# A softmax attention kernel: two and four of sixteen exponential blocks on VectorE in turn, one transposition step a unit, and a wait of GpSimd's product for VectorE's add

## The chip, the cores and the metric

The kernel runs on one core of a Trainium2 chip. The metric is the device time of one execution in microseconds (us), the median over several runs. A core has TensorE (PE in the profile; PEld is its loading of weights), VectorE (DVE), ScalarE (ACT), GpSimd (POOL) and SyncE (SP), each with a queue of its own that it works off in order. SBUF is the on-chip memory of all of them, PSUM the memory that TensorE writes its products to.

## The reference

Grouped-query attention: 32 query heads of 64 dimensions, 8 key and value heads, so four query heads share one of them. For each of 8 batches and 512 positions:

```python
batch, seq, n_heads, n_kv_heads, dim = 8, 512, 32, 8, 64
...
scores = np.einsum('bhqd,bhkd->bhqk', Q, K_expanded) * scale
weights = np.exp(scores - np.max(scores, axis=-1, keepdims=True))
weights = weights / (np.sum(weights, axis=-1, keepdims=True) + 1e-10)

output = np.einsum('bhqk,bhkd->bhqd', weights, V_expanded)
```

Inputs and output are float32.

## The kernel before

The kernel leaves the maximum out (exp without it gives the same quotient while nothing overflows) and checks on the way that the sums and V stay in bounds; if they do not, a slow general path recomputes everything. Here only the fast path runs.

**Units and jobs.** A unit is one batch and two of its key heads, with the eight query heads that use them: 32 units, four a batch. A unit is two jobs (64 in all, numbered j): job j has one key head and its four query heads as two pairs i = 0 and 1. The scores of a job are 16 blocks of 128 keys by 512 queries, and each block is to be exponentiated. Two blocks (m = 0, 1) share a PSUM tile of 128 × 1024.

**Two ways to the exponential.** ScalarE does most blocks: `act_tile(j, n)` has TensorE write scores to one of two PSUM tiles `s_ps`, and ScalarE writes exp of them to the SBUF tile `pt` (one ACTIVATE of 1024, or of 512 where a tile has a single block left). VectorE and GpSimd do the first blocks of pair 1, with integer arithmetic on the bits of a 16-bit float:

- `exp_d`: TensorE writes scores into `d_ps`, VectorE scales them to an integer `u`;
- `exp_d2`: VectorE masks the low ten bits, `f = u & 1023`, and, from job 3 to 62, GpSimd at once computes `g` (an add and a multiply of f) and the product `w = g * f` (`exp_d3`, `correction`);
- `exp_d4`: VectorE adds, `pt = u + w`, one job later.

`taken(j)` says how many blocks go this way: two, or three in even jobs from job 10 on (`WIDE`). With three, the third block has a scores matmul and a u of its own, issued at the end of the job before, and ScalarE's tile beside it has one block of 512 elements.

**The rest of a job.** While the scores of job j are made, TensorE multiplies the weights of job j−1 with V: `pv(last, 0, ...)` and `pv(last, 1, ...)`, each 32 matmuls into the one PSUM tile `pv`; a column of ones in V gives the sums. `norm(last, i)` then runs on VectorE: a reciprocal of the sums (L336) and a multiplication into `osb` (L340); SyncE stores a unit when its last norm is issued. `trans_q` transposes a job's queries on TensorE into `d_ps` (eight transposes) and VectorE copies them to `qt` (L167), for job j + 2. `check_v` (L173) reduces a chunk of V to its maximum, `check_sums` (L304) tests the collected reciprocals every eighth job.

**Order.** The order on each engine is the order in which the program is written (`tc.manual_schedule()`); semaphores follow from the tiles. In the main loop a job runs, on VectorE: u; norm of the last job's pair 0; the copy of queries; the add of the last job; f of this job; norm of pair 1. So f, and GpSimd's g and w behind it, follow the add, which has waited for the last job's w:

```python
        if late and by_pool(last):
            exp_d4(last)
        check_sums()
        exp_d2(j)
```

GpSimd also issues the loads of Q, K and V, ahead of its g and w in a job. SyncE transposes K by DMA at the start of a batch's third unit, and stores. PSUM: two tiles `s_ps`, one `d_ps` (for the scores of VectorE's blocks and for transposes by turns), one `pv`, two banks each.

Of the kernel before, what the change touches and what calls it, by code (L numbers as in the profile page):

```python
# [12 lines left out]
BF16 = mybir.dt.bfloat16  # L13
FP16 = mybir.dt.float16
# [3 lines left out]
ALU = mybir.AluOpType  # L18
# [15 lines left out]
V_HI = 1.0e15  # L34


WIDE = lambda j: j >= 10 and j % 2 == 0


@with_exitstack  # L40
# [18 lines left out]
def fast_path(ctx, tc, Q, K, V, out, flag):  # L59
    nc = tc.nc  # L60
    B, S, H, D = Q.shape
# [3 lines left out]
    GP = KV // 2  # L65
# [65 lines left out]
    def d_tile():  # L131
        return d_pool.tile([128, 2, S], FP32, name="d_ps")
# [3 lines left out]
    def first_k(gp, swap, bank):  # L136
# [8 lines left out]
                nc.tensor.transpose(ps[:, sc, :], kn[0][:, sc, h:h + 2, :], ident)  # L145
        return lambda: nc.vector.tensor_copy(out=kt_first[:, gp, swap, :], in_=half_bank)  # L146

    def dma_k(b):
        kt[b] = kt_pool.tile([128, 2, GP, S], BF16, name="kt")
        for sc in range(SC):  # L150
            nc.sync.dma_start_transpose(
                out=kt[b][:, 0, :, sc * 128:(sc + 1) * 128],
                in_=kn[b][:, sc, :, :].rearrange("p g d -> p (g d)"),
            )
        for to, of in ((0, 64), (64, 0)):
            nc.sync.dma_start(out=kt[b][to:to + 64, 1, :, :], in_=kt[b][of:of + 64, 0, :, :])

    def trans_q(j, bank, lo=0, hi=NPAIR):
        u, g = divmod(j, 2)
        ps = bank.bitcast(BF16).rearrange("p (i sc c) -> p i sc c", i=NPAIR, sc=SC)  # L160
        for i in range(lo, hi):
            for sc in range(SC):
                h = g * HPG + 2 * i
                nc.tensor.transpose(ps[:, i, sc, :], qn[u][:, sc, h:h + 2, :], ident)  # L164
        if u not in qt:
            qt[u] = qt_pool.tile([128, 2, NPAIR, S], BF16, name="qt")
        return lambda: nc.vector.tensor_copy(  # L167
            out=qt[u][:, g, lo:hi, :], in_=ps[:, lo:hi, :, :].rearrange("p i sc c -> p i (sc c)")
        )

    def check_v(b, sc):
        n = b * SC + sc
        nc.vector.tensor_reduce(  # L173
            out=okv[:, n:n + 1], in_=vt[b % 2][:, sc, :, 0:D], op=ALU.max, axis=AX.XY,
            apply_absolute_value=True,
        )
# [4 lines left out]
    DPAIR = NPAIR - 1  # L181

    def taken(j):
        return 3 if WIDE(j) else 2

    def act_tiles(j):
        every = [(i, kc, m) for i in range(NPAIR) for kc in range(SC) for m in range(2)]
# [19 lines left out]
    def open_job(j):  # L207
        pt = pt_pool.tile([128, NPAIR, SC, 2, S], FP16, name="pt")
        jobs.setdefault(j, {}).update(pt=pt, pv={})

    def act_tile(j, n):
        group = act_tiles(j)[n]
        i, kc, lo = group[0]
        ps = s_pool.tile([128, 2, S], FP32, name="s_ps")
        for _, _, m in group:
            scores(j, ps[:, m, :], i, kc, m)
        nc.scalar.activation(  # L217
            out=jobs[j]["pt"][:, i, kc, lo:, :], in_=ps[:, lo:, :], func=EXP, scale=scale
        )

    def exp_d(j, lo, hi, ps):
        st = jobs.setdefault(j, {})
        if "u" not in st:
            for name, dtype in (("u", I16), ("f", I16), ("g", BF16), ("w", BF16)):
                st[name] = dve_pool.tile([128, 3, S], dtype, name=name + "16")[:, 0:taken(j), :]
        for n in range(lo, hi):
            scores(j, ps[:, n - lo, :], DPAIR, n // 2, n % 2)
        return lambda: nc.vector.tensor_scalar(  # L228
            out=st["u"][:, lo:hi, :], in0=ps[:, 0:hi - lo, :], scalar1=A_U, scalar2=B_U,
            op0=ALU.mult, op1=ALU.add,  # L230
        )
# [7 lines left out]
    def correction(engine, f, g, w):  # L239
        as_bits = engine is nc.gpsimd  # L240
        engine.tensor_scalar(  # L241
            out=g, in0=f, scalar1=-EXP_F1, scalar2=EXP_K * 2.0 ** (24 * as_bits),
            op0=ALU.add, op1=ALU.mult,
        )
        engine.tensor_tensor(out=w, in0=g, in1=f.bitcast(FP16) if as_bits else f, op=ALU.mult)  # L245

    def exp_d2(j):
        st = jobs[j]
        nc.vector.tensor_single_scalar(  # L249
            out=st["f"], in_=st["u"], scalar=1023, op=ALU.bitwise_and  # L250
        )
        if by_pool(j):
            exp_d3(j, nc.gpsimd)

    def exp_d3(j, engine):
        st = jobs[j]
        correction(engine, st["f"], st["g"], st["w"])

    def exp_d4(j):
        st = jobs[j]  # L260
        n = taken(j)
        nc.vector.tensor_tensor(  # L262
            out=st["pt"][:, DPAIR, :, :, :].rearrange("p kc m q -> p (kc m) q")[:, 0:n, :].bitcast(
                U16
            ),
            in0=st["u"],
            in1=st["w"],
            op=ALU.add,
        )
# [8 lines left out]
    def pv(j, i, lo, hi):  # L278
        st = jobs[j]
        u, g = divmod(j, 2)  # L280
        b, gp = divmod(u, GP)
        if lo == 0:

            if j < NJOB - 1:
                t = pv_pool.tile([128, 2, S], FP32, name="pv")
            else:
                t = d_tile() if i == 0 else s_pool.tile([128, 2, S], FP32, name="s_ps")
            t = t.rearrange("p m (qc c) -> p m qc c", qc=SC)
            st["pv"][i] = t[:, :, :, 0:D + 1]
        order = blocks(j, i)  # L290
        for n in range(lo, hi):
            kc, m, qc = order[n]
            nc.tensor.matmul(  # L293
                st["pv"][i][:, m, qc, :],
                st["pt"][:, i, kc, m, qc * 128:(qc + 1) * 128],
                vt[b % 2][:, kc, 2 * gp + g, :],
                start=(n < 2 * SC and qc == 0),
                stop=(n >= len(order) - 2 * SC and qc == SC - 1),
            )
# [108 lines left out]
    trans_q(0, bank[:, 0, :], 0, 1)()  # L408


    for j in range(NJOB):
        end = j == NJOB - 1
        last = j - 1
        late = last >= 0
        u, g = divmod(j, 2)
        b, gp = divmod(u, GP)
        open_job(j)
        if j == 1:

            nc.gpsimd.tensor_copy(out=gate, in_=jobs[0]["pt"][0:1, 0, SC - 1, 0, 0:1])  # L420
            load_q(2)
            load_q(3)
        if g == 0 and u >= 1 and u + 3 < NU:
            load_q(u + 3)
        if (gp, g) == (1, 0) and b + 1 < B:
            load_k(b + 1)
        if 3 <= 2 * gp + g < 3 + SC and b + 1 < B:
            load_v(b + 1, chunks=(2 * gp + g - 3,))
        if gp == 2 and g == 0 and b + 1 < B:
            dma_k(b + 1)  # L430

        cut = (4, 18) if taken(j) > 2 else (11, 19)
        act_tile(j, 0)
        if j == 0:
            trans_q(0, bank[:, 1, :], 1, NPAIR)()
            act_tile(j, 1)
            exp_d(j, 0, 2, d_tile())()
        else:
            exp_d(j, 0, 2, d_tile())()
            act_tile(j, 1)  # L440

        if j == 8:
            check_v(0, 0)
        if g == (b < B - 1) and j > 1:
            check_v(b, gp)
        if late:
            pv(last, 0, 0, 16)
        act_tile(j, 2)
        if late:
            pv(last, 0, 16, 32)  # L450
            norm(last, 0)
        act_tile(j, 3)

        reads = []
        if not end:
            bank = d_tile()

            ahead = (j + 1,) if j < 7 else (8, 9) if j == 7 else (j + 2,)
            for n, to in enumerate(ahead):
                if to < NJOB:  # L460
                    reads.append(trans_q(to, bank[:, n, :]))
            if j == 1:
                for swap in range(2):
                    reads.append(first_k(1, swap, bank[:, 1, swap * S // 2:]))
            elif j > 1 and b == 0 and gp + 1 < GP:
                reads.append(first_k(gp + 1, g, bank[:, 1, :]))
        else:
            pv(j, 0, 0, 16)
        for read in reads:
            read()  # L470
# [5 lines that stand above are left out]
        if not by_pool(j):  # L476
            exp_d3(j, nc.vector)
            exp_d4(j)
        act_tile(j, 4)
        if late:  # L480
            pv(last, 1, 0, cut[0])
        act_tile(j, 5)
        if not end and taken(j + 1) > 2:
            exp_d(j + 1, 2, taken(j + 1), bank[:, 1:2, :])()
        if late:
            pv(last, 1, *cut)
        act_tile(j, 6)
        if late:
            pv(last, 1, cut[1], 32)
            norm(last, 1)  # L490
            del jobs[last]
        if end:
            pv(j, 0, 16, 32)
            norm(j, 0)
            pv(j, 1, 0, 32)
            norm(j, 1)
# [118 lines left out]
```

## Time and profile before

| | |
|---|---|
| median of three runs | 423.73 us (423.22 to 424.65) |
| span of the profiled execution | 422.0 us |
| ScalarE busy | 404.2 us, 96% |
| TensorE matmul busy | 385.7 us, 91% (ends modelled) |
| VectorE busy | 344.9 us, 82% |
| GpSimd busy | 291.8 us, 69% |
| mean granted TensorE clock | 0.984 |

The profiled execution's own time is its span of 422.0 us from the first to the last instruction; what lies around it is the difference to the runs' times, 1.7 us to their median. Busy shares are means over the whole span. In the steady part an even and an odd job together take 12.50 us: on GpSimd's timeline, g of three blocks starts at 206.21, and g of two blocks at 199.99 and again at 212.48.

### The profile page before, as it was taken

Reading aid. Unit: us, or ns where it says so; the run is one execution under the profiler, and the core shown is the slowest. Engines: PE = TensorE matmul, PEld = TensorE weight load, DVE = VectorE, ACT = ScalarE, POOL = GpSimd, SP = SyncE. Lnnn points to the kernel's source line nnn. Section 1 sums busy time; section 2 is a strip of 40 time slices with the busy share of each in tenths; the row PEclk is TensorE's granted clock in tenths of the full one; section 3 lists DMA queues with packets and bytes.
Section 4 is the critical chain, followed back from the end, with each engine's and each line's share of the span. In section 5 each row is a group of like instructions: output and inputs, shape, how many; then the busy total and the mean of one; then the engine's idle time right before and its main releaser. Section 6 shows DMA issues by size and latency. Waiting matters only on the chain.

```text
span 422.0 us, 13063 instructions
## 1 busy us (share of the span) xinstructions
PE 385.7 (91%) x5689; PEld 233.6 (55%) x5689; DVE 344.9 (82%) x611; ACT 404.2 (96%) x449; POOL 291.8 (69%) x209
## 2 busy tenths in 40 slices
PE   6889999999999999999999999999999999999983
PEld 2446565555555555555555555555555555555552
DVE  2697788889888888888888888888989888898875
ACT  3899999999999999999999999999999999999992
POOL 8504656778758876787866887677885887666560
PEclk9599999999999999999999999999999999999998
DMA  9996986599967998499964999649996799642223
GB/s 97 177 139 159 217 165 151 70 207 187 191 151 99 216 198 160 133 198 133 229 150 116 206 163 255 157 69 200 157 225 155 122 206 207 148 123 101 102 91 115
DMA packets 91438, 66.95 MB, mean 159 GB/s; under 512 B 52080, under 2 KB 74608, under 8 KB 91376
## 3 DMA queue, kind: packets, MB, share of 16 engines
q0 software_dynamic: 56544, 25.17, 51.1%
q1 hardware_dynamic: 34832, 40.90, 34.5%
q8 instruction: 45, 0.74, 0.7%
q14 instruction: 17, 0.14, 0.1%
HBM read 50.33 MB, written 33.55 MB: 199 GB/s over the span
## 4 chain that ended last, share of the span: by engine, by line
ACT 54%; PE 36%; DVE 6%; issue 1%; POOL 1%; ACTq 0%; DVEq 0%; POOLq 0%
ACT pt L217 54%; PE s_ps L199 17%; PE pv L293 16%; PE d_ps L199 1%; DVE o_sb L340 1%; PE d_ps L164 1%; DVE pt L262 1%; DVE u L228 1%; DVE qt L167 1%; DVE w L245 0%; POOL q_nat L126 0%; DVE kt_first L146 0%; ACTq L217 0%; PE d_ps L143 0%; DVE f L249 0%
## 5 line engine op out<-in xcount | busy, mean ns | idle before, releaser
L217 ACT ACTIVATE pt<-s_ps 128x1024 f16<-128x1024 f32 (+1 forms) x448 | 402.9, 1066 | 9.1 <-PE s_ps L199 9.0
L293 PEld LDWEIGHTS <-pt 128*128 128x128 f16 x4096 | 144.2, 98 | 86.8 <-issue 50.4
L293 PE MATMUL pv<-v,pt 128*128 128x65 bf16 x4032 | 183.2, 195 | 2.6 <-DVE o_sb L340 1.6
L199 PE MATMUL s_ps<-qt,kt 64*128 64x512 bf16 x757 | 152.7, 384 | 19.9 <-ACT pt L217 15.4
L245 POOL TENSOR_TENSOR w<-g,f 128x1024 bf16<-128x1024 bf16 (+1 forms) x60 | 153.7, 2562 | 5.0
L241 POOL TENSOR_SCALAR g<-f 128x1024 bf16<-128x1024 int16 (+1 forms) x60 | 73.9, 1231 | 110.1 <-DVE f L249 110.1
L228 DVE TENSOR_SCALAR u<-d_ps 128x1024 int16<-128x1024 f32 (+1 forms) x91 | 96.2, 1058 | 1.1 <-PE d_ps L199 1.1
L340 DVE TENSOR_TENSOR o_sb<-pv,inv 128x512 f32<-128x512 f32 x125 | 86.5, 692 | 4.5 <-DVE inv L336 0.2
L199 PEld LDWEIGHTS <-kt 64*128 64x128 bf16 x896 | 49.0, 93 | 62.6 <-issue 35.0
L336 DVE RECIPROCAL inv<-pv 128x8 f32<-128x8 f32 x125 | 25.9, 207 | 55.8 <-PE pv L293 55.4
L262 DVE TENSOR_TENSOR pt<-u,w 128x1536 uint16<-128x1536 int16 (+1 forms) x64 | 50.9, 795 | 0.2
L167 DVE COPY qt<-d_ps 128x1024 bf16<-128x1024 bf16 (+1 forms) x65 | 44.3, 683 | 4.5 <-PE d_ps L164 2.9
L164 PE MATMUL d_ps<-ident,q_nat 128*128 128x128 bf16 x512 | 40.1, 222 | 1.1 <-DVE kt_first L146 0.9
L164 PEld LDWEIGHTS <-q_nat 128*128 128x128 bf16 x512 | 29.2, 98 | 15.8 <-issue 15.7
L199 PE MATMUL d_ps<-qt,kt 64*128 64x512 bf16 x139 | 31.4, 376 | 0.3
L249 DVE TENSOR_SCALAR f<-u 128x1536 int16<-128x1536 int16 (+1 forms) x64 | 30.8, 481 | 0.0
L111 POOL DMA_DIRECT2D v<-in_V_dram x32 | 29.0, 910 | 0.4 <-issue 0.4
L126 POOL DMA_DIRECT2D q_nat<-in_Q_dram x34 | 27.4, 806 | 1.5 <-DMA q_nat<-in_Q_dram 1.3
L199 PE MATMUL s_ps<-qt,kt_first 64*128 64x512 bf16 x112 | 23.7, 419 | 4.1 <-ACT pt L217 3.0
L173 DVE TENSOR_REDUCE okv<-v 128x1 f32<-128x512 bf16 x32 | 21.6, 675 | 0.0
L199 PEld LDWEIGHTS <-kt_first 64*128 64x128 bf16 x128 | 8.0, 95 | 12.2 <-issue 8.4
L103 POOL DMA_DIRECT2D k_nat<-in_K_dram x10 | 7.7, 770 | 1.0 <-POOLq L599 0.8
(40 smaller groups left out, 37.6 us busy)
## 6 DMA issues: line engine op xcount, KB each, us to landing
out_dram<-o_sb SPq DMA_DIRECT2D x31, 1024.0 KB, 6.9
q_nat<-in_Q_dram POOLq DMA_DIRECT2D x31, 512.0 KB, 6.3
k_nat<-in_K_dram POOLq DMA_DIRECT2D x7, 512.0 KB, 8.6
v<-in_V_dram POOLq DMA_DIRECT2D x28, 128.0 KB, 7.6
kt<-kt SPq DMA_DIRECT2D x14, 256.0 KB, 4.6
out_dram<-o_sb SPq DMA_DIRECT2D x4, 256.0 KB, 2.4
kt<-k_nat SPq DMA_TRANSPOSE x28, 5.6
v<-in_V_dram POOLq DMA_DIRECT2D x4, 96.0 KB, 7.8
```

Source lines behind the costliest of these rows:

```text
L111: nc.gpsimd.dma_start(out=vt[b % 2][:, sc, lo:hi, 0:D], in_=V[b, sc * 128:(sc + 1) * 128, lo:hi, :],)
L164: nc.tensor.transpose(ps[:, i, sc, :], qn[u][:, sc, h:h + 2, :], ident)
L167: return lambda: nc.vector.tensor_copy(out=qt[u][:, g, lo:hi, :], in_=ps[:, lo:hi, :, :].rearrange("p i sc c -> p i (sc c)"))
L199: nc.tensor.matmul(ps, keys[64 * m:64 * m + 64, g ^ m, kc * 128:(kc + 1) * 128], qt[u][64 * m:64 * m + 64, g, i, :], start=True, stop=True,)
L217: nc.scalar.activation(out=jobs[j]["pt"][:, i, kc, lo:, :], in_=ps[:, lo:, :], func=EXP, scale=scale)
L228: return lambda: nc.vector.tensor_scalar(out=st["u"][:, lo:hi, :], in0=ps[:, 0:hi - lo, :], scalar1=A_U, scalar2=B_U, op0=ALU.mult, op1=AL ...
L241: engine.tensor_scalar(out=g, in0=f, scalar1=-EXP_F1, scalar2=EXP_K * 2.0 ** (24 * as_bits), op0=ALU.add, op1=ALU.mult,)
L245: engine.tensor_tensor(out=w, in0=g, in1=f.bitcast(FP16) if as_bits else f, op=ALU.mult)
L249: nc.vector.tensor_single_scalar(out=st["f"], in_=st["u"], scalar=1023, op=ALU.bitwise_and)
L262: nc.vector.tensor_tensor(out=st["pt"][:, DPAIR, :, :, :].rearrange("p kc m q -> p (kc m) q")[:, 0:n, :].bitcast(U16), in0=st["u"], in1=st ...
L293: nc.tensor.matmul(st["pv"][i][:, m, qc, :], st["pt"][:, i, kc, m, qc * 128:(qc + 1) * 128], vt[b % 2][:, kc, 2 * gp + g, :], start=(n < 2 ...
L340: nc.vector.tensor_tensor(out=osb[u][:, :, h:h + 2, :].rearrange("p qc m d -> p m qc d"), in0=sums[:, :, :, 0:D], in1=inv[:, :, :, None].t ...
```

## The change

From job 8 to job 62 two new functions take the place of the loop's body, `two_job` for even and `four_job` for odd jobs; the jobs before and the last one run as they did, with `WIDE` gone (two blocks each).

- VectorE and GpSimd take two blocks in an even job and four in an odd one (9 to 61), so ScalarE has seven whole tiles and six. In a four_job the blocks go in two halves of two: each has its own scores, u, f, g and w; one add of four blocks follows in the next job.
- f is issued ahead of the add of the last job, not behind it. GpSimd's w waits for that add by an extra dependency (`behind`): in a four_job the first half's w for the add of two blocks, in a two_job w for the add of four.
- The queries of both jobs of the next unit are transposed in the even job, into both banks of `d_ps`, with one copy of 2048 elements (`copy_unit`) in place of two of 1024.
- The loads of Q and K are issued at the end of the even job, and one chunk of V at the end of each odd one. `check_v` runs in the even job. `check_sums` stands behind the second f of an odd job.

```diff
-WIDE = lambda j: j >= 10 and j % 2 == 0
+FOUR = lambda j: 9 <= j < 63 and j % 2 == 1
...
+    def copy_unit(u, both):
+        nc.vector.tensor_copy(
+            out=qt[u].rearrange("p g i s -> p (g i s)"),
+            in_=both.bitcast(BF16).rearrange("p n s -> p (n s)"),
+        )
...
     def taken(j):
-        return 3 if WIDE(j) else 2
+        return 4 if FOUR(j) else 2
...
+    def behind(this, other):
+        if this is not None and other is not None:
+            tc.add_manual_dep(
+                this.ins,
+                other.ins.name,
+                mybir.DependencyInfo(mybir.DependencyClass.Sync, mybir.DependencyReason.DATA),
...
+            )
+
+    def two_job(j):
+        u, last = j // 2, j - 1
+        b, gp = divmod(u, GP)
+        act_tile(j, 0)
+        exp_d(j, 0, 2, d_tile())()
+        act_tile(j, 1)
+        check_v(b, gp)
+        pv(last, 0, 0, 16)
+        act_tile(j, 2)
+        pv(last, 0, 16, 32)
+        norm(last, 0)
+        act_tile(j, 3)
+        both = d_tile()
+        if u + 1 < NU:
+            trans_q(j + 2, both[:, 0, :])
+        act_tile(j, 4)
+        if u + 1 < NU:
+            trans_q(j + 3, both[:, 1, :])
+        w = exp_d2(j)
+        behind(w, exp_d4(last))
+        if u + 1 < NU:
+            copy_unit(u + 1, both)
+        act_tile(j, 5)
+        pv(last, 1, 0, 16)
+        act_tile(j, 6)
+        pv(last, 1, 16, 32)
+        norm(last, 1)
+        del jobs[last]
+        if u + 3 < NU:
+            load_q(u + 3)
+        if gp == 1 and b + 1 < B:
+            load_k(b + 1)
+
+    def four_job(j):
+        last = j - 1
+        b, gp = divmod(j // 2, GP)
+        act_tile(j, 0)
+        exp_d(j, 0, 2, d_tile())()
+        w = exp_d2(j, 0, 2)
+        act_tile(j, 1)
+        pv(last, 0, 0, 16)
+        act_tile(j, 2)
+        pv(last, 0, 16, 32)
+        norm(last, 0)
+        behind(w, exp_d4(last))
+        act_tile(j, 3)
+        exp_d(j, 2, 4, d_tile())()
+        exp_d2(j, 2, 4)
+        check_sums()
+        act_tile(j, 4)
+        pv(last, 1, 0, 16)
+        act_tile(j, 5)
+        pv(last, 1, 16, 32)
+        norm(last, 1)
+        del jobs[last]
+        if b + 1 < B:
+            load_v(b + 1, chunks=(gp,))
...
+        if 8 <= j < NJOB - 1:
+            if gp == 2 and g == 0 and b + 1 < B:
+                dma_k(b + 1)
+            (four_job if FOUR(j) else two_job)(j)
+            continue
```

More of the change, by code (lines that the diff above doesn't have):

```diff
@@ L159, in trans_q @@
         u, g = divmod(j, 2)
+        if j >= NJOB:
+            return lambda: None
         ps = bank.bitcast(BF16).rearrange("p (i sc c) -> p i sc c", i=NPAIR, sc=SC)
@@ L224, in exp_d @@
             for name, dtype in (("u", I16), ("f", I16), ("g", BF16), ("w", BF16)):
-                st[name] = dve_pool.tile([128, 3, S], dtype, name=name + "16")[:, 0:taken(j), :]
+                st[name] = dve_pool.tile([128, 4, S], dtype, name=name + "16")[:, 0:taken(j), :]
         for n in range(lo, hi):
@@ L244, in correction, with exp_d2, exp_d3 @@
         )
-        engine.tensor_tensor(out=w, in0=g, in1=f.bitcast(FP16) if as_bits else f, op=ALU.mult)
-    def exp_d2(j):
+        return engine.tensor_tensor(
+            out=w, in0=g, in1=f.bitcast(FP16) if as_bits else f, op=ALU.mult
+        )
+    def exp_d2(j, lo=0, hi=None, behind=None):
         st = jobs[j]
+        hi = taken(j) if hi is None else hi
         nc.vector.tensor_single_scalar(
-            out=st["f"], in_=st["u"], scalar=1023, op=ALU.bitwise_and
+            out=st["f"][:, lo:hi, :], in_=st["u"][:, lo:hi, :], scalar=1023, op=ALU.bitwise_and
         )
         if by_pool(j):
-            exp_d3(j, nc.gpsimd)
-    def exp_d3(j, engine):
+            return exp_d3(j, nc.gpsimd, lo, hi)
+    def exp_d3(j, engine, lo=0, hi=None):
         st = jobs[j]
-        correction(engine, st["f"], st["g"], st["w"])
+        hi = taken(j) if hi is None else hi
+        return correction(engine, *(st[n][:, lo:hi, :] for n in ("f", "g", "w")))
     def exp_d4(j):
@@ L261, in exp_d4 @@
         n = taken(j)
-        nc.vector.tensor_tensor(
+        return nc.vector.tensor_tensor(
             out=st["pt"][:, DPAIR, :, :, :].rearrange("p kc m q -> p (kc m) q")[:, 0:n, :].bitcast(
@@ L408, in fast_path @@
     trans_q(0, bank[:, 0, :], 0, 1)()
+    def behind(this, other):
[4 more added lines that the diff above has]
+                mybir.DependencyInfo(mybir.DependencyClass.Sync, mybir.DependencyReason.DATA),
+                reason="these two hold up each other when they meet",
+            )
+    def two_job(j):
[54 more added lines that the diff above has]
+            load_v(b + 1, chunks=(gp,))
     for j in range(NJOB):
@@ L430, in fast_path @@
             dma_k(b + 1)
-        cut = (4, 18) if taken(j) > 2 else (11, 19)
+        cut = (11, 19)
         act_tile(j, 0)
@@ L440, in fast_path @@
             act_tile(j, 1)
-        if j == 8:
+        if j == 6:
             check_v(0, 0)
-        if g == (b < B - 1) and j > 1:
+        if g == 1 and 1 < j < 8:
             check_v(b, gp)
@@ L456, in fast_path @@
             bank = d_tile()
-            ahead = (j + 1,) if j < 7 else (8, 9) if j == 7 else (j + 2,)
+            ahead = (j + 1,) if j < 7 else (8, 9)
             for n, to in enumerate(ahead):
@@ L482, in fast_path @@
         act_tile(j, 5)
-        if not end and taken(j + 1) > 2:
-            exp_d(j + 1, 2, taken(j + 1), bank[:, 1:2, :])()
         if late:
```

## The prediction

> **What bounds the kernel now.** I read the page's busy line first, then the groups by form, then ScalarE's timeline, then one pair of jobs (an even and an odd one) on VectorE and GpSimd, last the list of waits.
>
> ```profile
> PE 385.7 (91%) x5689; PEld 233.6 (55%) x5689; DVE 344.9 (82%) x611; ACT 404.2 (96%) x449; POOL 291.8 (69%) x209
> ```
>
> ScalarE is the candidate. Its timeline, cut to two windows (start, length, count):
>
> ```profile
> 200.37 5.27 ACT L217 ACTIVATE pt<-s_ps 128x1024 f16<-128x1024 f32 x6
> 204.88 6.35 ACT L217 ACTIVATE pt<-s_ps 128x512 f16<-128x512 f32 x7
> ```
>
> Five whole tiles lie between 200.37 and 204.88: 0.90 us from start to start. The second row starts with a half tile and ends at 211.23; its last tile is 1.09 long, so six steps take 5.26, five of them whole (4.51): a half tile takes 0.75. A pair of jobs has 13 whole tiles and a half: 12.5 us. A window of one pair (212.48 to 224.98) has ScalarE busy for 12.50 of 12.50 us, VectorE for 10.49: ScalarE sets the pace.
>
> Prices, from the groups by form (busy us, mean ns | idle before):
>
> ```profile
> L245 POOL TENSOR_TENSOR w<-g,f 128x1024 bf16<-128x1024 bf16 x33 | 70.1, 2125 | 2.8
> L167 DVE COPY qt<-d_ps 128x1024 bf16<-128x1024 bf16 x63 | 43.5, 692 | 3.1 <-PE d_ps L164 1.5 <-PE d_ps L143 1.3 <-PE d_ps L145 0.3
> L241 POOL TENSOR_SCALAR g<-f 128x1024 bf16<-128x1024 int16 x33 | 34.3, 1039 | 66.7 <-DVE f L249 66.7
> L167 DVE COPY qt<-d_ps 128x512 bf16<-128x512 bf16 x2 | 0.8, 424 | 1.4 <-PE d_ps L164 1.4
> ```
>
> VectorE over the pair, in order of time:
>
> ```profile
> 201.58 1.21 DVE L228 TENSOR_SCALAR u<-d_ps 128x1024 int16<-128x1024 f32 x1
> 203.48 0.21 DVE L336 RECIPROCAL inv<-pv 128x8 f32<-128x8 f32 x1 [0.69 <-PE pv L293]
> 203.72 0.69 DVE L340 TENSOR_TENSOR o_sb<-pv,inv 128x512 f32<-128x512 f32 x1
> ...
> 204.96 0.68 DVE L262 TENSOR_TENSOR pt<-u,w 128x1024 uint16<-128x1024 int16 x1
> 205.56 0.55 DVE L249 TENSOR_SCALAR f<-u 128x1536 int16<-128x1536 int16 x1
> ...
> 207.87 1.22 DVE L228 TENSOR_SCALAR u<-d_ps 128x1024 int16<-128x1024 f32 x1
> 209.00 0.68 DVE L173 TENSOR_REDUCE okv<-v 128x1 f32<-128x512 bf16 x1
> 209.62 0.21 DVE L336 RECIPROCAL inv<-pv 128x8 f32<-128x8 f32 x1
> 209.86 0.69 DVE L340 TENSOR_TENSOR o_sb<-pv,inv 128x512 f32<-128x512 f32 x1
> 210.49 0.69 DVE L167 COPY qt<-d_ps 128x1024 bf16<-128x1024 bf16 x1
> 211.10 0.95 DVE L262 TENSOR_TENSOR pt<-u,w 128x1536 uint16<-128x1536 int16 x1
> 211.97 0.42 DVE L249 TENSOR_SCALAR f<-u 128x1024 int16<-128x1024 int16 x1
> 212.30 0.69 DVE L228 TENSOR_SCALAR u<-d_ps 128x512 int16<-128x512 f32 x1
> ```
>
> Back to back, an instruction costs the distance to the next start: u 1.13, V check 0.62, reciprocal and norm 0.87, copy 0.61, add (L262) 0.60 on two blocks and 0.87 on three, mask f (L249) 0.33 on two. The order matters: now f always comes behind the add, which waits for GpSimd's product of the job before, so no f and no add ever runs beside a GpSimd g or w. Once, in job 0, an f met another GpSimd instruction, the issue of a Q load (two rows, of VectorE's and of GpSimd's timeline):
>
> ```profile
> 12.78 0.71 DVE L249 TENSOR_SCALAR f<-u 128x1024 int16<-128x1024 int16 x1
> 12.51 0.76 POOL L126 DMA_DIRECT2D q_nat<-in_Q_dram  x1
> ```
>
> It took 0.71 instead of 0.42: held 0.29 of the 0.49 that the issue still had to run.
>
> **The change part by part.** From job 9 on VectorE takes four blocks in odd jobs (27 of them, 9 to 61) and two in even ones.
>
> ScalarE: each odd job loses a whole tile (−0.90), each even one has its half tile made whole (+0.15): −0.75 a pair, 27 pairs, −20 us, if nothing else binds. The pair would be 13 × 0.90 = 11.7.
>
> VectorE, a pair after: three u (3.39), one check (0.62), four norms (3.48), three f (0.99), adds of two and four blocks (0.60 + 1.14, by 0.27 a block from 0.60 and 0.87), one copy of 2048 for two of 1024 (0.61 + 2 × 0.27, the step between the rows of 512 and 1024: 1.15). Sum 11.37. To that come waits for TensorE: a norm's end at 201.66 (201.58 overlaps its tail) is followed by the next reciprocal at 203.48, 1.82 later, since the products have one PSUM tile. In the odd job only u and f lie between two norms (they cover 1.40: wait 0.42), in the even one u and the check (1.69: wait 0.13). The bounds check of the sums, two of 0.29 every four pairs, adds 0.14. Together 12.06: VectorE alone is already above ScalarE's 11.7.
>
> GpSimd, a pair after: three times g and w, 3 × (1.04 + 2.13), and a Q and a V issue (0.82, 0.88 in its timeline): 11.2, with some 0.07 between two instructions 11.8. It is full as well.
>
> The new meeting. In the odd job the add of job j−1 releases w of the first half (the new wait). Behind that waiting w stand GpSimd's g and w of the second half and the V issue; VectorE's next large add waits for them, and TensorE's second products for that. (In the even job w waits for the large add in the same way, with the Q issue and the odd job's g behind it; there g runs beside the add, and w is late by 0.1 only.) VectorE goes on at once: u of the second half 0.60 behind the add's start, f of the second half at 1.73. But w runs from 0.68 + 0.09 (the lag seen between f and g) to 2.90. So f meets a w with 1.17 to run, in every pair, and u cannot fill more. What that costs no row shows: the bounds are nothing (the rows of u, norm, copy and reduce beside w show no stretch: L340 has 692 ns everywhere; less than nothing is excluded, since a meeting frees no time) and 1.2 (f waits w out). The one f that met GpSimd was held; scaled as in its row (0.29 of 0.49) it would lose 0.7. I take the full wait, since w reads and writes SBUF all along, where an issue need not. Cost 1.2, on VectorE's path, and g, w of the second half start that much later. A second meeting: f of the even job comes as the V issue runs: 0.29 as in the row (from 0 to 0.29).
>
> Forecast: 12.06 + 1.2 + 0.29 = 13.55 a pair against 12.50: 1.05 × 27 = 28. The profiled execution is 422.0 of span, and the median of the runs, 423.7, lies 1.7 above it, which stays: 450.4 of span, 452 in all.
>
> The Trainium skill, "SBUF — State Buffer", section "Who interferes with whom", speaks against this change: a one-source VectorE instruction that uses both port pairs, and a GpSimd instruction, exclude each other for the whole length of the one that came first. By that rule f's cost at w is the full 1.2 as well, and the sum the same; the row of 12.78 agrees in kind only. The same section counts a VectorE instruction with two SBUF inputs against a GpSimd one that reads SBUF; that is the third rival.
>
> The rest: TensorE does the same products, 16 transposes at once in even jobs and none in odd ones; with pairs of 12 us and more it has slack (11.74 busy in 12.50, pipelined ends included). The Q load is issued at the end of the even job, not its beginning; it is used two pairs later. The K issue (landing 8.6) sits between w and g of the first half, where GpSimd has 0.7 to spare before the add. SyncE's K transposes then wait some us at the start of the third unit, with only that unit's store behind them. The V issue moves behind the second w: the last chunk of a batch starts some 4.5 before TensorE needs it (f, the large add, the copy, a norm and half a first product stand between) and lands in 3.5 at best, as in the row of V issues (3.5/7.8/14.6 from least to most, the long ones beside a Q load, which now lies half a pair away); if late by 0.5, six times, 3 us.
>
> **Rivals.** (1) Nothing is held. For it: every other instruction beside w is unstretched; against: the row at 12.78. Then VectorE's 12.06 and the loop through GpSimd (the large add waits for the second w: 0.2 more) give 12.3, 0.2 × 27 = 5 less: 418. It decides if the two holds together lose under 0.4.
> (2) ScalarE still binds: 11.7 a pair, 403. Against it: VectorE's sum; it needs reciprocals that wait for nobody.
> (3) Slower still: the add meets g too. In the even job the large add starts just before g, which then begins at 1.27 instead of 0.17; w ends 1.1 later, f of the odd job's first half and its g follow, and the add of two blocks must wait g out: 0.5 more, 14.05 a pair, 42 over: 466. The add has met issues only, at a loss of 0.01 (959 against 948). By the Trainium skill's rule for two SBUF inputs this is what happens. It decides once g waits over half a us.
> (4) Each meeting costs 0.29 and no more: 12.06 + 2 × 0.29 = 12.64 a pair, 4 more: 428; if the wait for w covers part of it, no change.
>
> **How the numbers follow.** Forecast 0.43, (3) 0.23, (4) 0.14 (a third of it no change), (1) 0.13, (2) 0.07. A measurement of this kernel tells about 0.3%, 1.3 us, from no change. Faster 0.20, same 0.05, slower 0.75. The range leaves out (2) and what lies above 469: from 416 to 469. The forecast's own range, f held for 0.7 to 1.4, is 438 to 457.
>
> **What would show it.** On L249's line (now exp_d2's), the second f of each odd job at some 1.6 us; a pair of about 13.5 on VectorE's timeline; ScalarE idle about 1.8 a pair (13.55 − 11.7), waiting for PE s_ps, whose scores stand behind products that wait for VectorE. 421 activations, all whole. Unstretched f means (1); f at 0.7, (4); g late behind the large add, (3). An f held and yet a pair under 12.5 would say that VectorE's sum is wrong.

## The result: slower by a tenth

The changed kernel takes 467.4 us (median; 466.8 to 473.7) against 423.8: a ratio of 1.106 (95% interval 1.099 to 1.112). The forecast was 452 in a range of 416 to 469. The page of the profiled execution (span 465.0, run of 466.8) begins:

```profile
PE 386.5 (83%) x5689; PEld 236.1 (51%) x5689; DVE 411.3 (88%) x611; ACT 394.6 (85%) x422; POOL 362.6 (78%) x263
...
PEclk8799999988979898999997899999999999979978
...
PE 53%; DVE 34%; issue 5%; ACT 4%; POOL 1%; DMA 1%; ACTq 0%; DVEq 0%; POOLq 0%
```

ScalarE has lost the 27 tiles (421 activations and the table load) but is idle for 70 us; the chain that ended last, 54% on ScalarE before, now has 4% of it. TensorE's granted clock, 0.98 on average before, is 0.93: the second line shows it dipping all along the span. An undisturbed pair on VectorE, from the odd job's first f to the next large add (starts and lengths in us):

```profile
214.26 0.43 DVE L260 TENSOR_SCALAR f<-u 128x1024 int16<-128x1024 int16 x1
...
215.79 0.86 DVE L274 TENSOR_TENSOR pt<-u,w 128x1024 uint16<-128x1024 int16 x1
216.57 1.21 DVE L236 TENSOR_SCALAR u<-d_ps 128x1024 int16<-128x1024 f32 x1
217.82 1.38 DVE L260 TENSOR_SCALAR f<-u 128x1024 int16<-128x1024 int16 x1
219.13 0.19 DVE L348 RECIPROCAL inv<-pv 128x8 f32<-128x8 f32 x1
...
222.58 0.42 DVE L260 TENSOR_SCALAR f<-u 128x1024 int16<-128x1024 int16 x1
222.91 1.22 DVE L274 TENSOR_TENSOR pt<-u,w 128x2048 uint16<-128x2048 int16 x1
```

GpSimd beside it:

```profile
215.07 1.03 POOL L249 TENSOR_SCALAR g<-f 128x1024 bf16<-128x1024 int16 x1
216.80 2.12 POOL L253 TENSOR_TENSOR w<-g,f 128x1024 bf16<-128x1024 bf16 x1 [0.69 <-DVE pt L274]
219.29 1.04 POOL L249 TENSOR_SCALAR g<-f 128x1024 bf16<-128x1024 int16 x1 [0.37 <-DVE f L260]
...
222.49 0.99 POOL L111 DMA_DIRECT2D v<-in_V_dram  x1
223.56 1.47 POOL L249 TENSOR_SCALAR g<-f 128x1024 bf16<-128x1024 int16 x1
```

The second f starts at 217.82, in the middle of w, and ends at 219.20, 0.28 after w's end at 218.92: it ran only when w was over, 0.96 late. The f of the even job (222.58) meets the V issue and is not held. The add of two blocks (215.79) meets a g and takes 0.86, elsewhere up to 1.05, instead of 0.68; the g of 223.56 meets the large add and takes 1.47 instead of 1.04. The previous large add started at 209.74, so this pair took 13.17 us. Two things lengthen a pair at full clock. One is the K issue: the pair of these rows, between the large adds of 196.10 and 209.74, took 13.64:

```profile
200.37 0.98 POOL L126 DMA_DIRECT2D q_nat<-in_Q_dram  x1
201.35 0.75 POOL L103 DMA_DIRECT2D k_nat<-in_K_dram  x1
...
203.63 2.12 POOL L253 TENSOR_TENSOR w<-g,f 128x1024 bf16<-128x1024 bf16 x1
```

Here w starts 3.26 after the Q issue instead of 2.79, and the second f, at 203.81, takes 2.22; the add of two blocks meets no g and takes 0.68. The other is the check of the sums in the odd job, behind the second f:

```profile
191.03 1.35 DVE L316 SCALAR_TENSOR_TENSOR ok<-inv,ok 128x128 f32<-128x128 f32 x2
192.30 0.19 DVE L348 RECIPROCAL inv<-pv 128x8 f32<-128x8 f32 x1
```

Its two instructions hold VectorE for 1.27 us; the kernel before takes 0.61 for both. At full clock the pair with the check takes 14.45 (large adds at 294.24 and 308.69). What waits for all this is TensorE, and ScalarE for TensorE (engine, line, released by: us, times, longest):

```profile
PEld L305 <- DVE o_sb L352: 75.3, 89, 3.1
ACT pt L225 <- PE s_ps L207: 61.0, 60, 6.3
```

Over the 26 intervals between large adds the mean pair is 14.05 us: 13.2 in undisturbed stretches at full clock, up to 15.5 where the check and the half clock come together. 27 pairs at 1.55 above 12.50 are 42 of the 43.6 us.

### The profile page after: what moved, and what is told of

Same layout as the page of the kernel before. It is cut to its first block, busy times and chain, and to the rows that moved or that the text cites. A ratio compares the mean times of both kernels' runs of the same rounds, so it can differ in the third digit from the quotient of the medians.

```text
span 465.0 us, 13113 instructions
## 1 busy us (share of the span) xinstructions
PE 386.5 (83%) x5689; PEld 236.1 (51%) x5689; DVE 411.3 (88%) x611; ACT 394.6 (85%) x422; POOL 362.6 (78%) x263
## 4 chain that ended last, share of the span: by engine, by line
PE 53%; DVE 34%; issue 5%; ACT 4%; POOL 1%; DMA 1%; ACTq 0%; DVEq 0%; POOLq 0%
PE pv L305 26%; PE s_ps L207 18%; DVE f L260 9%; PE d_ps L172 8%; DVE u L236 7%; DVE o_sb L352 7%; DVE pt L274 5%; ACT pt L225 4%; DVE inv L348 3%; DVE ok L316 2%; DMA v<-in_V_dram 1%; DVE w L253 0%; POOL w L253 0%; POOL q_nat L126 0%; DVE qt L175 0%
## 5 line engine op out<-in xcount | busy, mean ns | idle before, releaser
L225 ACT ACTIVATE pt<-s_ps 128x1024 f16<-128x1024 f32 x421 | 393.4, 1055 | 61.3 <-PE s_ps L207 61.0
L305 PE MATMUL pv<-v,pt 128*128 128x65 bf16 x4032 | 175.6, 198 | 51.2 <-DVE o_sb L352 48.6
L253 POOL TENSOR_TENSOR w<-g,f 128x1024 bf16<-128x1024 bf16 x87 | 184.7, 2123 | 22.3 <-DVE pt L274 17.0
L249 POOL TENSOR_SCALAR g<-f 128x1024 bf16<-128x1024 int16 x87 | 110.5, 1270 | 62.0 <-DVE f L260 59.9
L236 DVE TENSOR_SCALAR u<-d_ps 128x1024 int16<-128x1024 f32 x91 | 110.5, 1214 | 1.1 <-PE d_ps L207 1.1
L260 DVE TENSOR_SCALAR f<-u 128x1024 int16<-128x1024 int16 x91 | 67.4, 741 | 1.9
L274 DVE TENSOR_TENSOR pt<-u,w 128x1024 uint16<-128x1024 int16 x64 | 62.5, 976 | 0.2
L172 PE MATMUL d_ps<-ident,q_nat 128*128 128x128 bf16 x512 | 45.6, 241 | 1.1 <-DVE kt_first L146 0.9
L149 DVE COPY qt<-d_ps 128x2048 bf16<-128x2048 bf16 x27 | 32.9, 1220 | 2.8 <-PE d_ps L172 2.4
L175 DVE COPY qt<-d_ps 128x1024 bf16<-128x1024 bf16 (+1 forms) x11 | 7.0, 642 | 4.7 <-PE d_ps L172 3.3
```

The costliest lines, as they stand in the source:

```text
L149: nc.vector.tensor_copy(out=qt[u].rearrange("p g i s -> p (g i s)"), in_=both.bitcast(BF16).rearrange("p n s -> p (n s)"),)
L225: nc.scalar.activation(out=jobs[j]["pt"][:, i, kc, lo:, :], in_=ps[:, lo:, :], func=EXP, scale=scale)
L236: return lambda: nc.vector.tensor_scalar(out=st["u"][:, lo:hi, :], in0=ps[:, 0:hi - lo, :], scalar1=A_U, scalar2=B_U, op0=ALU.mult, op1=AL ...
L249: engine.tensor_scalar(out=g, in0=f, scalar1=-EXP_F1, scalar2=EXP_K * 2.0 ** (24 * as_bits), op0=ALU.add, op1=ALU.mult,)
L253: return engine.tensor_tensor(out=w, in0=g, in1=f.bitcast(FP16) if as_bits else f, op=ALU.mult)
L260: nc.vector.tensor_single_scalar(out=st["f"][:, lo:hi, :], in_=st["u"][:, lo:hi, :], scalar=1023, op=ALU.bitwise_and)
```

## The experiments

"Changed kernel" is the kernel after; times are medians, each ratio against the kernel before on the same chip.

**1. Without the second f.**

```diff
-        exp_d2(j, 2, 4)
+        st = jobs[j]
+        correction(nc.gpsimd, st["f"][:, 0:2, :], st["g"][:, 2:4, :], st["w"][:, 2:4, :])
```

> The changed kernel with the second mask f of each odd job left out (GpSimd's second g and w read the first half's f; so these two blocks get a wrong correction of a few per cent). In the changed kernel's trace this f takes 1.38 us in an undisturbed pair of 13.17 us: 0.42 of work and 0.96 of being held by the first w. Theory V (the hold lies on VectorE's path, as the prediction has it): 1.3 us a pair go, and with them most of the half-clock stretches of TensorE; ScalarE's 11.7 or VectorE's work of 11.9 binds: 408 to 425 us. Theory G (what binds is GpSimd's loop of turns with VectorE: its three g and w, its issues, and the masks and adds that exclude them): only the 0.37 us in which GpSimd waits for this f go: 12.8 a pair and 450 to 460 us.

Measured: 445.1 us, 1.051 (1.048 to 1.054), between the two. An undisturbed pair falls from 13.17 to 12.55 only, because the hold turns up one step later, at the even job's f:

```profile
308.55 1.37 DVE L260 TENSOR_SCALAR f<-u 128x1024 int16<-128x1024 int16 x1
309.85 1.21 DVE L274 TENSOR_TENSOR pt<-u,w 128x2048 uint16<-128x2048 int16 x1
...
321.11 1.37 DVE L260 TENSOR_SCALAR f<-u 128x1024 int16<-128x1024 int16 x1
322.40 1.21 DVE L274 TENSOR_TENSOR pt<-u,w 128x2048 uint16<-128x2048 int16 x1
```

VectorE now arrives 0.96 early there, while the second w still runs. Neither theory had that.

**2. The second f behind the norm.**

```diff
-        exp_d2(j, 2, 4)
         check_sums()
...
         norm(last, 1)
+        exp_d2(j, 2, 4)
```

> The changed kernel with the second f of each odd job (and the g and w behind it) issued after the norm of pair 1 instead of before it: f then comes as the first w ends, nothing of the work is left out. Theory V: the hold of 0.96 us leaves VectorE's path, 12.2 a pair, TensorE's clock recovers: 420 to 435 us. Theory G: GpSimd's loop is as long as before, 13.1 a pair: 455 to 468 us.

Measured: 446.0, 1.053 (1.051 to 1.054). All the work is there, only the place of one f (and of the g and w behind it) differs, and 21 us of the loss are gone. Undisturbed pairs take 12.86, which is 0.31 less and makes 8 us; much of the rest goes with the clock, which is 0.967 here against 0.930 (run 12 tries that alone). Again the holds move:

```profile
313.89 1.06 DVE L274 TENSOR_TENSOR pt<-u,w 128x1024 uint16<-128x1024 int16 x1
...
316.84 0.67 DVE L260 TENSOR_SCALAR f<-u 128x1024 int16<-128x1024 int16 x1
...
319.99 1.15 DVE L260 TENSOR_SCALAR f<-u 128x1024 int16<-128x1024 int16 x1
```

So the held f was on the path (theory V), but taking it off does not free VectorE for long. Six pairs of this run take 14.2 to 14.3; they are those with the check, and the pairs with the K issue take 13.3 at full clock.

**3. Without the second w.** GpSimd's last product of the odd job is replaced by g alone; f keeps its place.

```diff
-        exp_d2(j, 2, 4)
+        st = jobs[j]
+        nc.vector.tensor_single_scalar(out=st["f"][:, 2:4, :], ... op=ALU.bitwise_and)
+        nc.gpsimd.tensor_scalar(out=st["w"][:, 2:4, :], in0=st["f"][:, 2:4, :], ...)
```

> The changed kernel with GpSimd's product of the second half left out (g writes w's place, scaled small, so these two blocks get no correction). VectorE's work and the meeting of f with the first w stay. Theory V: f is still held 0.96 us on VectorE's path, so an undisturbed pair stays near 13.1 and the time at 455 to 467 us. Theory G: 2.2 us go from GpSimd's loop, the next bound is VectorE's path of some 12.2 to 12.6: 420 to 440 us.

Measured: 467.5, 1.105 (1.101 to 1.110): 2.1 us a pair less on GpSimd, and no change. The second f (its own line here) is held as ever:

```profile
L480 DVE TENSOR_SCALAR f<-u x27: 1381/1384/2225, 75.6 to 448.2; 128x1024 int16<-128x1024 int16 x27
```

Least, median and longest are those of the changed kernel. With the f where the change put it, GpSimd's load is not what binds: theory G falls for the changed kernel.

**4. Transposes in every job again.** As before the change: eight transposes and a copy of 1024 in each job.

> The changed kernel with the transposition undone: eight transposes and a copy of 1024 in every job instead of sixteen and one copy of 2048 in the even one. Rival theory T (TensorE's queue binds in the even job, where the chain of waits runs through 7.9 us of its products and transposes in a row): 0.55 us a pair go from that stretch, 12.6 a pair, 450 us or less. Theories V and G: TensorE only follows; VectorE has 0.07 us more work a pair and a copy of 0.61 in the odd job ahead of the norm: no change to 0.6 us a pair more, 465 to 485 us.

Measured: 502.3, 1.185 (1.182 to 1.188), worse than anybody said. The odd job now needs the one `d_ps` tile three times, and TensorE's queue stands while VectorE, behind the adds and holds, empties it:

```profile
PE d_ps L172 <- DVE u L236: 64.4, 27, 2.5
```

That is 2.4 us in each odd job. The transposition at once made room for the second scores. Theory T's forecast of 450 us or less failed, but the new wait covers what the run was to test: whether transposes in the even job cost time stays open here. In the changed kernel they are on the chain that ended last, as part of what TensorE does behind the norm:

```profile
219.35 0.70 DVE o_sb L352
220.10 0.67 PE pv L305 x16
...
222.02 0.55 PE d_ps L172 x8
```

**5. Both: f behind the norm, and no second w.**

> The second f behind the norm (as in e2_f_after_norm, which took 446.0 us, 12.86 an undisturbed pair) and GpSimd's second product left out as well (those two blocks get no correction). In e2_f_after_norm the second w still ran when the even job's f came, and held it to 1.14 us; the add of two blocks was held to 1.05 by a g. Theory B (a budget: f and the adds of VectorE and g and w of GpSimd never run at once, so their sum, some 12.6 us a pair, is the floor once no hold is wasted): without that w the sum is 10.5, the even job's f is free, and what binds is VectorE's own 12 us or ScalarE's 11.7: 415 to 430 us. Theory V2 (the holds hardly matter now; VectorE's work and the one PSUM tile of the products bind): no change, 440 to 447 us.

Measured: 429.5, 1.015 (1.009 to 1.020); 12.12 an undisturbed pair. At the even job's f the hold is gone, since no w runs there: it takes 0.42 again. The second f is still held to 0.67 in most pairs. VectorE's own work of about 12 us now nearly fills the pair.

```profile
308.39 0.42 DVE L260 TENSOR_SCALAR f<-u 128x1024 int16<-128x1024 int16 x1
308.72 1.22 DVE L274 TENSOR_TENSOR pt<-u,w 128x2048 uint16<-128x2048 int16 x1
...
320.51 0.42 DVE L260 TENSOR_SCALAR f<-u 128x1024 int16<-128x1024 int16 x1
320.84 1.22 DVE L274 TENSOR_TENSOR pt<-u,w 128x2048 uint16<-128x2048 int16 x1
```

Theory B (turns that exclude each other) forecast this time. The turns of a four-and-two pair are three g (3.12), three w (6.37), three f (1.26) and two adds (1.90): 12.65 us. Run 2 needs 12.86. Before, with five blocks, they were 7.73 and 2.60: 10.3 of 12.50. But 12.65 is no floor. Run 2 has a pair of 12.56 with all these turns, near its end, where no loads are issued any more:

```profile
414.48 1.21 DVE L274 TENSOR_TENSOR pt<-u,w 128x2048 uint16<-128x2048 int16 x1
...
427.04 1.21 DVE L274 TENSOR_TENSOR pt<-u,w 128x2048 uint16<-128x2048 int16 x1
```

The lengths overlap at their ends; counted from start to start as the prediction counts (f 0.33, adds 0.60 and 1.14) the turns are 12.2. And run 3, whose turns are 2.1 fewer, is no faster than the changed kernel: there the sum does not set the pair.

**6. As 2, with the K issue and the check of the sums moved.** `load_k` behind the odd job's last w, `check_sums` behind its first f.

> As e2_f_after_norm, with the issue of the K load moved behind the odd job's last w (where a g waits for the large add anyway) and the bounds check of the sums moved behind the odd job's first f. In the trace of e2_f_after_norm the pair with the K issue takes 14.2 us and those with the check or a V chunk 13.3 to 13.6, against 12.86 for an undisturbed one. Theory B: six K pairs lose 1.3 us each and seven check pairs some 0.4: 434 to 439 us. If the extra time of those pairs comes from the transfers themselves (K's landing, stores) and not from GpSimd's issue: 444 to 448 us.

Measured: 438.4, 1.033 (1.029 to 1.036). The expectation has the two kinds of pair the wrong way round: in run 2 the pairs of 14.2 are those with the check. Moved, the check costs next to nothing where nothing else waits: two of its six pairs take 12.85 and 12.89, against 12.85 for an undisturbed one. The K issue nearly keeps its price: in the pair behind it the first w starts 2.62 behind the large add instead of 2.20, and the pair takes 13.28, 0.43 more than an undisturbed one. So the gain is the check's. In the other four check pairs TensorE waits for a V chunk, and they take 13.25 to 16.67 in the profiled execution, the slowest of the five (443.4); in the longest the chunk lands 7 us after its issue, on the chain. Late V chunks were the prediction's small risk.

```profile
PE pv L305 <- DMA v<-in_V_dram: 6.5, 4, 3.1
```

**7. Two blocks always.** `FOUR` is never true; order, transposition, wait and loads as in the change.

> The changed kernel's order with two blocks in every job (no four): the transposition at once, the extra wait, f ahead of the add and the moved loads remain. Theory B: no f meets a w, ScalarE binds with 14 whole tiles a pair, 12.64 us against the kernel before's 12.50: 426 to 429 us. If the transposition or the new order costs by itself: 432 us or more.

Measured: 432.6, 1.021 (1.017 to 1.025), 4 above the window. ScalarE is busy without a break, as expected, but its tiles come slower, 30 of them in this row:

```profile
301.95 27.86 ACT L225 ACTIVATE pt<-s_ps 128x1024 f16<-128x1024 f32 x30
```

(27.86 − 1.09) / 29 = 0.92 a tile instead of 0.90, which makes 12.9 a pair and the rest of the time. Why a tile costs 0.02 more in this order was not found. The change's frame without the four blocks thus loses 9 us: 4 of them (0.14 a pair) by the half tile that is whole again, the rest by the slower tiles.

**8. Four blocks in every second unit.** As run 2, with four in the odd jobs of units 0 and 2 of a batch and two elsewhere; check in the odd jobs between.

> Four blocks in the odd job of every second unit only (units 0 and 2 of a batch), two in all others; the second f behind the norm, the check of the sums in the odd jobs of the units between, where the K issue lies too. As many blocks leave ScalarE as before the change, all its tiles whole: 24.4 us for two pairs against 25.0, so 416 us if the units between give GpSimd and VectorE the time to catch up. Theory B allows it (10.6 us a pair on average). If a four pair's 12.86 is not made good in the next pair, two pairs take 25.5: 430 us.

Measured: 430.5, 1.016 (1.013 to 1.020). ScalarE's 14 tiles are saved, but undisturbed two pairs take 25.00 (large adds at 259.38 and 284.38), exactly what the kernel before takes, and not 24.4. Two pairs with the check and the K issue take 26.06, and six of these make 6.4 of the 6.8 us lost. There the check met a g and a w and took 3.3 us for both its instructions:

```profile
290.67 3.34 DVE L316 SCALAR_TENSOR_TENSOR ok<-inv,ok 128x128 f32<-128x128 f32 x2
```

**9. Products to keep the clock up, first try.** 32 products of zeros in each even job, into unused columns of the tile `pv`.

> The changed kernel with 32 products of zeros more in every even job from 10 on, 63 columns each, into unused columns of the products' PSUM tile, at the place where TensorE waits some 2 us for the norm behind the held f. They lengthen nothing that is waited for. Theory C (a part of the loss is TensorE's clock: its idle time halves the clock for 3.4 us at a time, and the chain of waits runs through its products): the granted clock goes from 0.93 to 0.97 or more, and the pairs that now take 14.5 to 15.5 come down to 13.2 to 13.7 (but for the K pairs): 450 to 460 us. If the half clock falls only into time that TensorE would wait anyway: the clock rises and the time stays at 465 to 470 us.

Measured: 498.2, 1.176 (1.173 to 1.179). The tile's dependency made them wait for the norm themselves, so they did not run in idle time:

```profile
PE pv L442 <- DVE o_sb L354: 49.5, 27, 2.8
```

The question stays open here, but one thing follows: 1.1 us more of TensorE behind that norm lengthens an undisturbed pair by 1.1 (14.30). The path runs through the norm and on into TensorE.

**10. The add ahead of f in the even job.**

```diff
-        w = exp_d2(j)
-        behind(w, exp_d4(last))
+        exp_d4(last)
+        exp_d2(j)
```

> The changed kernel with the add of four blocks ahead of f in the even job, as before the change, so that g of that job never meets the add (in the changed kernel's trace g is held there until the add's end, 1.47 or 1.93 us instead of 1.04). Rival 3 (that hold is half a us of the path): 0.3 to 0.5 us a pair less, 450 to 458 us. If VectorE's path through the odd job's held f sets the pair and GpSimd has time in the even one: no change, 463 to 470 us.

Measured: 471.6, 1.111 (1.106 to 1.116). Now g is never held by the large add (1.04 at 340.35 in its trace), and nothing is gained. The first link of rival 3 happens, as the trace of the changed kernel shows, but taking it away gains nothing.

**11. The kernel before, with four blocks in every fourth job.** In its old order, so that f, g and w never meet.

```diff
-WIDE = lambda j: j >= 10 and j % 2 == 0
+WIDE = lambda j: j >= 10 and j % 4 == 2
...
-        return 3 if WIDE(j) else 2
+        return 4 if WIDE(j) else 2
...
-            exp_d(j + 1, 2, taken(j + 1), bank[:, 1:2, :])()
+            exp_d(j + 1, 2, taken(j + 1), d_tile())()
```

> The kernel before, in its own order (add, then f, then g and w, which so never meet), with four blocks in every fourth job instead of three in every second, and two in the others. ScalarE keeps as many blocks and has only whole tiles: 27 of 0.903 for two pairs, 24.4 us against 25.0. By the budget (g and w of six blocks, f and the adds) a four pair needs some 12.6 us in turns, and the pair behind it 8.9, together less than 24.4. Theory B: ScalarE stays the bound, 415 to 418 us. If the late add of four blocks (w of 4 us ends some 1.3 us later than w of three) stalls TensorE for more than ScalarE's two tiles cover: 420 us or more.

Measured: 454.3, 1.071 (1.069 to 1.074). A row of its VectorE timeline (start in us, length, operation, the wait before it):

```profile
223.41 1.22 DVE L262 TENSOR_TENSOR pt<-u,w 128x2048 uint16<-128x2048 int16 x1 [1.66 <-POOL w L245]
```

The product that it waited for, in its GpSimd timeline:

```profile
219.31 4.06 POOL L245 TENSOR_TENSOR w<-g,f 128x2048 bf16<-128x2048 bf16 x1
```

The old order avoids every meeting by going one after the other, and with four blocks that line is too long: the add comes 1.7 late and TensorE's queue with it. Theory B, which allowed 415 to 418, misses here, as in runs 7 and 8. The clock, 0.930 as in the changed kernel, may have a part in the loss; that was not tried, and neither were two halves in the old order.

**12. Products to keep the clock up, second try.** 24 products of zeros into the scores tile that the even job's third tile uses next; they wait for ScalarE only.

```diff
+        third = s_pool.tile([128, 2, S], FP32, name="s_ps")
+        for n in range(24 if j >= 10 else 0):
+            nc.tensor.matmul(third[:, n % 2, 0:D + 1], warm[:, 0:128], warm[:, 0:D + 1], ...)
         pv(last, 0, 0, 16)
-        act_tile(j, 2)
+        act_tile(j, 2, third)
```

> The question of e9_filler again, whose extra products waited for the norm themselves (same PSUM tile) and so lay on the path, 1.11 us a pair. Now 24 products of 65 columns of zeros go into the scores tile that the even job's third tile will use; they wait for ScalarE's first tile only, in time that TensorE spends waiting for the norm behind the held f. Theory C (the half clock is part of the loss): the granted clock rises from 0.93 to 0.97 or more, and the pairs of 14.5 to 15.5 us fall to 13.2 to 13.7, but for those with a K load: 450 to 460 us. If the half clock only fills waiting time: the clock rises and the time stays at 465 to 470 us. If the clock follows longer means than single gaps: it stays at 0.93 and so does the time.

Measured: 453.6, 1.071 (1.067 to 1.075): more work, 14 us less. The granted clock is 0.986, and its row is flat:

```profile
PEclk8799999999999999999999999999999999999998
```

Nearly every pair is now regular: 13.15 undisturbed (large adds at 216.19 and 229.34), 13.62 with the K issue, 14.43 with the check, 13.55 on average. Theory C holds. The changed kernel's own trace agrees: its longest stretch at full clock, 133 us, holds four pairs on end, from the add of 294.24 to that of 348.67, that take 13.61 on average, with one K issue and one check among them. In run 12 four such pairs take 13.59.

No kernel beat the one before; the best with all the work done is run 8.

## Why the prediction was right, and where its sum was off

**Direction and mechanism: right.** The second f meets the first w in every pair and waits it out, on VectorE's path. That f ends 0.28 after w in all 27 odd jobs of the changed kernel, and moving that one instruction returns 21 us (run 2), part of them by the clock. It agrees with the Trainium skill, "SBUF — State Buffer", section "Who interferes with whom": the one that comes second waits for the whole of the first.

**The sum came out, and the time did not, for a step that it left out.** The forecast's 13.55 a pair is what the changed kernel takes when TensorE keeps its clock (run 12: 13.55, 453.6 us against 452 forecast). That it meets so closely is luck, as the terms below show. The step that failed is "with pairs of 12 us and more it has slack": TensorE's slack became idle time, the clock fell (13 stretches at half clock, 67 us in all, against 2 and 16 before; one at the start and one at the end are in both), and since the chain runs through its products behind each norm, half speed there is lost time: 14 us. That the time came out at rival 3's 466 is a coincidence.

**Inside the 13.55, terms were off both ways.** By run 12, an undisturbed pair of 13.15 against 13.41 (the forecast less 0.14 for the check):
- f at w: 0.96, not 1.2. When f starts, w has 1.10 to run, and f's 0.42 overlap w's end by 0.14.
- f at the V issue: nothing, not 0.29. The issue itself takes 0.99 instead of 0.88.
- The add of two blocks: up to 0.37 held by g. The prediction had this only in rival 3, as the end of a chain that begins with the large add. Run 10 removed that beginning and the add was still held, 1.15 at the most in its trace: it meets g by the odd job's own order.
- The K issue: 0.47 in each of six pairs, where nothing was planned. The "0.7 to spare" are there (w waits 0.69 for the add in an undisturbed pair), but the issue and its gap take 0.83, the g behind it meets the add and takes 1.37 instead of 1.04, and so w starts 0.47 later and f waits for longer. Run 6, which moved the issue, did not take this away.
- The check of the sums: 1.28 a time where 0.58 was planned. Its second instruction takes 1.03 instead of 0.29 beside a g, and with the first it stands on VectorE's path behind the held f. Run 6, which moved it, took most of this away.

27 × 0.65, six times 1.28 and six times 0.47 are 28 us, the difference between run 12 and the kernel before within 2. Without the two holds, of 0.96 and some 0.36, the undisturbed pair would be 11.8, less than the 12.50 before: by this estimate from the rows the holds cost an undisturbed pair its gain.

**The rivals.** (1), nothing held, falls with the 1.38 us of every second f, and (4), 0.29 a meeting, with the same row. (2), ScalarE still binding, falls with its 70 us of idle time. (3) is right in that adds and g hold each other, and the add's hold is on the path; it is wrong in the chain that it draws, since taking away the first link gains nothing (run 10).

**What the prediction could have had.** It added up each engine. The sum over both engines of what can't run at once, 12.2 to 12.65 a pair against 10.3 before, would have said that hardly any room is left beside a period of 12.50. It would not have given the time: runs 3, 7, 8 and 11 do not follow it. In runs 1 and 2 the hold moved to the next f or add; whether another order avoids the loss is open.

## What to carry to other kernels

Before work is handed from one engine to two others, add up what these two can only do in turns, as if they were one engine; where that sum comes near the period, expect holds. An instruction that is held costs where it stands, and it may be a small one: here a check of two short instructions cost 1.28 each time, more than the issue of a load (0.47), and moving it took most of that away. And when TensorE starts to wait, look at the granted clock first: idle time that nobody misses can still be paid for in half speed.

## What the runs showed of the hardware that was not expected

- **The clock falls for short idle times.** In the changed kernel the longest single wait of TensorE in the list of waits is 3.1 us, and between start and end the clock still halved 11 times, which it never did before the change. The Trainium skill, "TensorE: Matmul & The Clock Gate", section "HAM oscillation — how this bites in real kernels", warns of idle gaps above some 3.4 us; here shorter ones were enough. 24 small products of zeros a pair, about a us, kept the clock at full speed. How much idle time it takes was not tried.
- **A held instruction shows as a long one.** No wait is listed: f is 1.38 or 2.22 us of "busy" VectorE, and the adds 0.86 to 1.05. VectorE's 88% contain these holds. Only the form's spread, 416 ns at the least and 2220 at the most for one shape, gives them away.
- **A meeting with a DMA issue differs from case to case.** The f of job 0 lost 0.29 to a Q issue that had begun 0.27 earlier; the f at 222.58 lost nothing to a V issue that had begun 0.09 earlier, and the issue took 0.1 longer; the f at 214.26, 0.25 behind the start of a Q issue, lost nothing either. What decides is open.
